# Differential attention: joining the two softmax halves one unit later, with scores one unit ahead

## The chip, the cores and the metric

The kernel runs on one core of a Trainium2 chip. The metric is the device time of one execution in microseconds (us). It is a whole two-layer network; the change lies in one phase of it, the attention of layer 0.

## The reference, cut to what matters

The network has two layers (layer 0 differential attention, layer 1 a state-space mixer), each followed by a dense MLP, over 1024 latent tokens and 256 context tokens. The attention has 8 heads; each head has two sets of queries and keys (c = 0, 1), two softmaxes, and one set of values:

```python
def attend(q, k, v):
    s = jnp.einsum('bqhcd,bkhcd->bhcqk', q, k).astype(jnp.float32)
    p = jax.nn.softmax(s, axis=-1)
    w = p[:, :, 0] - lam * p[:, :, 1]
    o = jnp.einsum('bhqk,bkhe->bqhe', w.astype(v.dtype), v)
    return rmsnorm(o, subln_g) * (1.0 - lambda_init)
```

Context queries see the 256 context keys, latent queries all 1280 keys. All is float32.

## The kernel before, in words

To keep float32 accuracy, products are done on TensorE (PE) with operands split into a high and a low part: `mm3` (lines 132 to 134) issues high x high, high x low and low x high. The split is a copy on ScalarE (ACT, L137) and a subtraction (L138) on VectorE (DVE) or GpSimd (POOL).

`phase_b` is the attention. A head is nine *units* of queries: u = 0 is the 256 context queries (two tiles of 128 with 256 keys each), u = 1 to 8 are 128 latent queries with 1280 keys each. Units pair up into five pairs of 256 queries: pair 0 is u = 0, pair 1 is u = 1 and 2, and so on to pair 4 (u = 7 and 8). The loop runs over n = 0 to 76: 72 units of eight heads, and five more to drain. In one turn of it several units are worked on:

- `scores` (L514, L520) of unit n: 12 matmuls (8 narrow ones for u = 0) into five banks of PSUM, half c = 0 in columns 0 to 1279, half c = 1 in 1280 to 2559.
- `maxima` (L529, L533) on DVE copies each half to SBUF (p0, p1) and takes its maximum; `exps` (L540, L543) on ACT does the exponentials in place, with their sums; `combine` (L551 to L554) on DVE joins the halves into p0. p0 has two buffers, p1 one.
- `w_part` transposes the joined weights of the unit before (`prev`) on PE (L566; L561 for u = 0) in three parts: four tiles into bank 5, two into the upper half of bank 6 (`pb`), four into bank 7, or bank 5 where a projection uses bank 7. `w_evac` brings them into wT: part 0 by ACT and DVE (L574, L575), parts 1 and 2 by a copy on ACT (L579) and a split on POOL (L580, L581).
- `values` of a pair: 30 matmuls (6 for pair 0) from wT and the values into the lower half of bank 6, once both units of the pair are in wT. The list `todo` sets when: two units after the pair's last unit. In these units (`late`) the evacuation is put behind the exponentials, since wT is still being read.
- `pair_out` (L662, L663) copies and squares the result; a unit later `pair_sums` (L669) sums the squares on PE into columns 256 and 257 of bank 6, which part 1 of the transposes also uses, and L670 copies them out.
- the projections of the next head's keys and queries, `proj_group`, in the units u = 0 (two), 2, 3, 5 and 7 (the table `AHEAD`): their 24 matmuls fill the gaps between the transposes (`fills`), in bank 7. Four are 512 columns wide, two 256. Afterwards come L466 on ACT and L467 on DVE (L461 and L462 for the narrow ones), a swap by DMA, POOL L472, DVE L475, and the split and store (L137, L138) some units later (`post`).
- norms of the head before the last (`norm_load`, `norm_calc`, `norm_rows`, `norm_pair` with L694), and for head 7 a part of the output product (`wo_group`) in ten units.

The order of PE, DVE, ACT and POOL within the phase is the order of the program text (`manual`). The DMAs are all issued on one queue (SP, line 80) whose order a scheduler chooses; a DMA there waits for its data, and those behind it wait with it. Keys have three buffers (`Kr`), queries two (`Qr`).

## Time and profile before

| what | us |
|---|---|
| three runs | 2940.19, 2940.97, 2946.08 |
| median | 2940.97 |
| profiled execution, first to last instruction (span) | 2929.2 |
| attention phase in the span (from the first scores of head 0) | 239.7 to about 907 |
| busy in the span: PE, DVE, ACT, POOL | 2739.6, 2021.3, 1367.5, 1062.1 |

The profile is of one execution; of that execution only the span is given. Matmuls are pipelined in the trace: a matmul's own time is longer than the distance to the next one's start, so durations on PE are read from starts. The profile's columns for a stretch of time are its length, the busy time of PE, the weight loads (PEld), DVE, ACT and POOL with the number of instructions, the clock granted to PE (1 is full), the share of DMA and its GB/s. In a timeline row stand start, duration, engine, line, operation, operands and count, and in brackets the idle time before it and who ended it.

### The profile page before, as it was taken

To read this page: it belongs to the slowest core of one execution; us is meant where nothing else is said; L and a number is where in the kernel's file an instruction comes from. 1 tells how busy PE (TensorE), PEld (TensorE's weight loads), DVE (VectorE), ACT (ScalarE), POOL (GpSimd) and SP (SyncE) were. 2 spreads that over 40 slices of the span, in tenths; PEclk is the share of its full clock that TensorE was granted. 3 is DMA by queue.
4 is the path that set the end of the run, shared out by engine and by line. 5 is a ranking of instruction groups with operands and counts; after the bars stand their busy time and mean duration, and the time that the engine had idled before them with its cause. 6 is when DMAs were issued, how large, how long until landed. Compare 5 with 4: busy or idle time off the path is not lost.

```text
span 2929.2 us, 43646 instructions
## 1 busy us (share of the span) xinstructions
PE 2739.6 (94%) x15200; PEld 2287.5 (78%) x15200; DVE 2021.3 (69%) x2956; ACT 1367.5 (47%) x2555; POOL 1062.1 (36%) x923
## 2 busy tenths in 40 slices
PE   5998999999988999999999999688899899999999
PEld 3687888788777887878877778588788678878887
DVE  5355777777764477676688768699743687758566
ACT  3424555555553663333444435377543643345443
POOL 2213666666553700000020004499410543326324
PEclk8999999999989999999999999899999999999999
DMA  9956455555744448886699988468834254467544
GB/s 250 292 181 205 139 164 169 162 149 162 220 145 152 140 152 303 303 291 243 228 299 293 274 241 258 153 200 264 282 124 136 72 175 159 148 213 256 159 139 141
DMA packets 454122, 588.44 MB, mean 201 GB/s; under 512 B 62742, under 2 KB 299532, under 8 KB 450700
## 3 DMA queue, kind: packets, MB, share of 16 engines
q1 hardware_dynamic: 453900, 585.63, 63.6%
q8 instruction: 120, 1.97, 0.3%
q14 instruction: 102, 0.84, 0.1%
HBM read 398.48 MB, written 182.82 MB: 198 GB/s over the span
## 4 chain that ended last, share of the span: by engine, by line
PE 66%; DMA 12%; DVE 10%; issue 4%; ACT 4%; SPq 2%; POOL 2%; DVEq 0%; ACTq 0%; POOLq 0%
PE PS L132 19%; PE PS L133 18%; PE PS L134 18%; SPq L80 2%; PE PS L520 2%; PE PS L1797 2%; ACT F L543 2%; PE PS L1832 1%; PE PS L566 1%; DVE F L533 1%; DVE R L138 1%; DVE H L138 1%; PE PS L202 1%; DMA U<-in_mlp_w 1%; DMA U<-Aa 1%
## 5 line engine op out<-in xcount | busy, mean ns | idle before, releaser
L132 PE MATMUL PS<-H 128*128 128x512 f32 x1048 | 412.0, 395 | 7.7 <-DVE FD L1604 5.0
L133 PE MATMUL PS<-H 128*128 128x512 f32 x1048 | 410.4, 392 | 0.0
L134 PE MATMUL PS<-H 128*128 128x512 f32 x1048 | 409.8, 392 | 0.0
L132 PE MATMUL PS<-H,R 128*128 128x512 f32 (+1 forms) x836 | 311.2, 378 | 18.5 <-ACT F L579 13.7
L133 PE MATMUL PS<-H,R 128*128 128x512 f32 (+1 forms) x836 | 303.8, 363 | 1.1 <-POOL H L138 1.1
L134 PE MATMUL PS<-H,R 128*128 128x512 f32 (+1 forms) x836 | 303.6, 364 | 0.0
L137 ACT ACTIVATE R<-W 128x512 fp32r<-128x512 f32 (+1 forms) x203 | 142.9, 711 | 208.7 <-PE PS L133 114.9
L132 PEld LDWEIGHTS PS<-H 128*128 128x128 f32 x1048 | 197.9, 189 | 52.4 <-DVE FD L1604 5.3
L134 PEld LDWEIGHTS PS<-H 128*128 128x128 f32 x1048 | 197.7, 189 | 42.5 <-issue 1.0
L133 PEld LDWEIGHTS PS<-H 128*128 128x128 f32 x1048 | 197.9, 189 | 41.2 <-issue 1.2
L132 PE MATMUL PS<-R,H 128*128 128x512 f32 x532 | 214.7, 407 | 7.4 <-ACT H L137 6.0
L543 ACT ACTIVATE F<-F,stat 128x1280 f32<-128x1280 f32 x128 | 174.3, 1362 | 83.8 <-DVE F L533 83.5
L133 PE MATMUL PS<-R,H 128*128 128x512 f32 x532 | 210.8, 397 | 0.0
L134 PE MATMUL PS<-R,H 128*128 128x512 f32 x532 | 208.3, 395 | 0.0
L137 ACT ACTIVATE H<-U 128x640 fp32r<-128x640 f32 x216 | 132.8, 677 | 144.2 <-PE PS L133 110.7
L132 PEld LDWEIGHTS PS<-H,R 128*128 128x128 f32 x836 | 160.7, 193 | 47.6 <-ACT F L579 15.1
L138 DVE TENSOR_TENSOR H<-W,H 128x512 fp32r<-128x512 f32 (+1 forms) x137 | 128.6, 949 | 93.6 <-ACT H L137 93.6
L138 DVE TENSOR_TENSOR R<-W,R 128x512 fp32r<-128x512 f32 (+1 forms) x166 | 150.8, 915 | 60.8 <-ACT R L137 53.5
L533 DVE TENSOR_SCALAR_CACHE_REDUCE F<-PS 128x1280 f32<-128x1280 f32 x128 | 185.1, 1482 | 9.1 <-PE PS L520 8.9
L138 DVE TENSOR_TENSOR H<-U,H 128x640 fp32r<-128x640 f32 x216 | 163.4, 793 | 39.5 <-ACT H L137 39.3
L580 POOL TENSOR_SCALAR R<-F 128x256 fp32r<-128x256 f32 (+1 forms) x128 | 122.8, 959 | 172.1 <-ACT F L579 149.1
L134 PEld LDWEIGHTS PS<-H,R 128*128 128x128 f32 x836 | 160.7, 192 | 25.9 <-issue 0.8
(477 smaller groups left out, 6818.0 us busy)
## 6 DMA issues: line engine op xcount, KB each, us to landing
W<-in_mlp_w SPq DMA_DIRECT2D x184, 256.0 KB, 3.1
U<-Aa SPq DMA_DIRECT2D x108, 320.0 KB, 5.0
Aa<-FU SPq DMA_DIRECT2D x91, 320.0 KB, 4.6
Ad<-F SPq DMA_DIRECT2D x112, 256.0 KB, 3.2
W<-Ad SPq DMA_DIRECT2D x112, 256.0 KB, 2.8
W<-in_ada_w SPq DMA_DIRECT2D x32, 512.0 KB, 6.9
FU<-in_mlp_w SPq DMA_DIRECT2D x32, 512.0 KB, 6.3
Ta<-FU SPq DMA_DIRECT2D x16, 1024.0 KB, 5.6
```

What stands on the lines that cost most here:

```text
L80: return self.nc.sync.dma_start(out=out, in_=in_)
L132: mm(out, ah, bh, start=first, stop=False, **kw)
L133: mm(out, ah, bl, start=False, stop=False, **kw)
L134: mm(out, al, bh, start=False, stop=last, **kw)
L137: self.nc.scalar.activation(hi, src, AF.Copy)
L138: (lo_eng or self.nc.vector).tensor_tensor(lo, src, hi.bitcast(F32), ALU.subtract)
L202: self.nc.tensor.matmul(acc[32 * j : 32 * j + 32, 0:256], self.scT[:, 2 * k : 2 * k + 32], w[:, 256 * j : 256 * j + 256], start=k == 0, st ...
L520: mm(self.PS[:, 1280 * c + k0 : 1280 * c + k1], Q[:, c, r, qs], K[c][:, k0:k1], start=r == 0, stop=r == 1)
L533: ts(p[c], self.PS[:, 1280 * c : 1280 * c + 1280], 1.0, None, ALU.mult, ALU.min, accum_out=sm[:, c : c + 1])
L543: nc.scalar.activation(p[c], p[c], AF.Exp, bias=sm[:, c : c + 1], scale=-1.0, accum_out=sn[:, 0:1] if c else s0[:, u + 1 : u + 2])
L580: nc.gpsimd.tensor_scalar(hi, t, 1.0, 0.0, ALU.mult, ALU.add)
L1797: mm(b[:, o : o + 160], X[:, d, i, 64 * j : 64 * j + 128], U[:, 4 * n + i, cols], start=True, stop=True)
```

## The change

- The joining of the halves (`combine`) of unit n moves to unit n + 1, ahead of that unit's maxima. The transposes move from one unit behind to two (`prevs`), the value products from n + 2 to n + 3, and the sums and norms with them by one unit; the loop has 78 turns in place of 77.
- `scores` of unit n + 1 stand at the end of turn n on PE, behind its transposes and fills, in place of those of unit n at its start.
- The evacuations stand in the same order in all units (`late` is gone).
- p0 has three buffers, keys have four, and the loads of keys and queries are put at other units to match. The two pools grow by 5 KB a partition each.

```diff
--- before.py
+++ after.py
@@ -616,13 +616,13 @@
 
     def phase_b(self):
         nc, mm = self.nc, self.nc.tensor.matmul
-        p0 = Ring([self.view(self.F1, 5 * i, (1280,)) for i in range(2)])
-        p1 = self.view(self.F1, 10, (1280,))
-        self.wraw = Ring([self.view(self.F1, 15 + 2 * i, (512,)) for i in range(3)])
+        p0 = Ring([self.view(self.F1, 5 * i, (1280,)) for i in range(3)])
+        p1 = self.view(self.F1, 15, (1280,))
+        self.wraw = Ring([self.view(self.F1, 20 + 2 * i, (512,)) for i in range(3)])
         o = self.fv(6, 256)
         sq = self.adat
         self.raw = Ring([self.wv(0, 1024)])
-        Kr = Ring([self.view(self.R1, 5 * i, (1280,)) for i in range(3)])
+        Kr = Ring([self.view(self.R1, x, (1280,)) for x in (0, 5, 10, 20)])
         Vr = Ring([self.rv(36 + 5 * i, 10, 128) for i in range(3)] + [self.view(self.R1, 15, (10, 128))])
         Qr = Ring([self.rv(51 + 4 * i, 2, 2, 256) for i in range(2)])
         self.wT = self.rv(16, 10, 256), self.rv(26, 10, 256)
@@ -630,7 +630,7 @@
         loaded = {}
 
         def load_k(h, c):
-            K = loaded[h, "k", c] = self.rv(0, 1280) if (h, c) == (7, 1) else Kr.next()
+            K = loaded[h, "k", c] = Kr.next()
             for k0, k1 in ((0, 256), (256, 1280)):
                 self.dma(K[:, k0:k1].bitcast(F32), self.Kd[h % 2, c, :, k0:k1])
 
@@ -753,8 +753,8 @@
             if u == 0:
                 self.oT = self.hgroups()
                 nc.vector.memset(ones, 1.0)
-            if u < 2:
-                wsplit6(u + 1)
+            if u in (0, 2):
+                wsplit6(u // 2 + 1)
             for g, k0, k1 in {0: ((2, 0, 6),), 1: ((0, 0, 3),), 2: ((0, 3, 6),), 3: ((1, 0, 3),), 4: ((1, 3, 6),)}.get(u, ()):
                 c0 = (256, 768, 0)[g]
                 for k in range(k0, k1):
@@ -786,7 +786,7 @@
         load_q(0, 1)
         load_v(0)
         units = [(h, u) for h in range(8) for u in range(9)]
-        prev, todo, sums, post, tail, run7 = None, [], [], [], [], []
+        prevs, joined, todo, sums, post, tail, run7 = [None, None], None, [], [], [], [], []
         split = self.proj_weights(1, 1)
         split(0)
         wts = {1: split(1)}
@@ -802,48 +802,54 @@
             while ready:
                 self.w_evac(*ready.pop(0))
 
+        def unit_args(h, u):
+            return u, loaded[h, (u + 1) // 2], (loaded[h, "k", 0], loaded[h, "k", 1])
+
         with self.manual():
-            for n in range(72 + 5):
+            self.scores(*unit_args(0, 0))
+            for n in range(72 + 6):
                 h, u = units[n] if n < 72 else (8, 9)
+                prev = prevs.pop(0)
                 front = n < 72
                 groups = []
                 pv = todo.pop(0)[1:] if todo and todo[0][0] == n else None
-                late = pv and pv[1]
                 parts = 3 if prev and prev[1] else 1 if prev else 0
-                if front and n - 6 >= 9 and (n - 6) % 9 < 5 and (n - 6) // 9 < 7:
-                    norm_load((n - 6) // 9 - 1, (n - 6) % 9)
+                if front and n - 7 >= 9 and (n - 7) % 9 < 5 and (n - 7) // 9 < 7:
+                    norm_load((n - 7) // 9 - 1, (n - 7) % 9)
                 if h == 7 and u > 5:
                     load6(u)
                 if front:
-                    K = loaded[h, 'k', 0], loaded[h, 'k', 1]
                     pair = (u + 1) // 2
-                    Q = loaded[h, pair]
                     s0 = hst[:, 0, h]
                     p, sn, sm = (p0.next(), p1), self.stat.next(), self.stat.next()
                     if u == 5 and h < 7:
                         load_v(h + 1)
                         load_k(h + 1, 0)
-                    if u % 2 == 0 and u < 8 and (h, pair + 1) not in loaded:
+                    if u == 6 and h < 7:
+                        load_k(h + 1, 1)
+                    if u in (1, 3, 5):
                         load_q(h, pair + 1)
+                    if u == 8 and h < 7:
+                        load_q(h + 1, 0)
+                        load_q(h + 1, 1)
                     if h < 7:
                         groups = [self.proj_group(h + 1, *a, wts[a[0]]) for a in self.AHEAD.get(u, ())]
                     if len(groups) == 2:
                         for f in groups[0][0] + groups[0][1]:
                             f()
-                    self.scores(u, Q, K)
-                    if u == 8 and h < 7:
-                        load_k(h + 1, 1)
-                        load_q(h + 1, 0)
-                        load_q(h + 1, 1)
+                if joined:
+                    self.combine(*joined)
+                    joined = None
+                if front:
                     self.maxima(u, p, sm)
-                if front:
+                    joined = u, p, s0, sn
                     if h < 7:
                         if u == 0:
                             qsplit = self.proj_weights(h + 1, 0)
                         if u == 5 and h < 6:
                             ksplit = self.proj_weights(h + 2, 1)
-                if 65 <= n < 75:
-                    groups = [wo_group(wo_order[n - 65])]
+                if 66 <= n < 76:
+                    groups = [wo_group(wo_order[n - 66])]
                 fills = [[], [], []]
                 if h >= 7 and groups:
                     fills = [groups[0][0][i : i + 2] for i in (0, 2, 4)]
@@ -856,27 +862,24 @@
                         tb = pb[:, 256:512] if part == 1 else self.bank(7 if part == 2 and not groups else 5)
                         t = self.w_part(prev[1], prev[2], part, tb)
                         ready.append((*t, part == 0))
-                    if not late or part == 2:
-                        evac()
+                    evac()
                     if part == 1:
                         next_post()
                     if front and part < 2:
                         self.exps(u, part, p, sm, s0, sn)
-                    if front and part == 1:
-                        self.combine(u, p, s0, sn)
-                    if late and part == 1:
-                        evac()
                     if part == 0:
                         todo7, run7 = run7, []
                         for f in todo7:
                             f.pop(0)()
                             if f:
                                 run7.append(f)
-                    if part == (2 if n < 73 else 0):
+                    if part == (2 if n < 74 else 0):
                         while sums and sums[0][0] <= n:
                             sums.pop(0)[1]()
                     for f in fills[part]:
                         f()
+                if n < 71:
+                    self.scores(*unit_args(*units[n + 1]))
                 if pv:
                     pair_out(*pv)
                     sums.append((n + 1, lambda a=pv: pair_sums(*a)))
@@ -894,17 +897,18 @@
                 if u == 8 and h < 6:
                     wts[1] = wk
                 if front and u % 2 == 0:
-                    todo.append((n + 2, h, pair))
-                prev = (h, u, p[0]) if front else None
+                    todo.append((n + 3, h, pair))
+                prevs.append((h, u, p[0]) if front else None)
                 if 0 < h < 8:
-                    if u == 3:
+                    step = u - 3 - (h < 7)
+                    if step == 0:
                         newton = norm_calc(h - 1)
-                    elif u == 4:
+                    elif step == 1:
                         newton()
-                    elif u == 5:
+                    elif step == 2:
                         norm_rows(h - 1)
-                if h < 8 and n - 6 >= 9 and (n - 6) % 9 < 5 and (n - 6) // 9 < 7:
-                    norm_pair((n - 6) // 9 - 1, (n - 6) % 9)
+                if h < 8 and n - 7 >= 9 and (n - 7) % 9 < 5 and (n - 7) // 9 < 7:
+                    norm_pair((n - 7) // 9 - 1, (n - 7) % 9)
                 if n == 72:
                     self.raw = Ring([self.wv(8, 1024), self.wv(12, 1024)])
                     self.wo_raws = [self.wo_load(3, 0), self.wo_load(0, 1)]
@@ -2227,7 +2231,7 @@
                     self.raw = Ring([self.wv(4 * i, 1024) for i in range(4)] + [self.f0(24.5 + 4 * i, 1024) for i in range(4)])
                     self.phase_v()
                 with pool("r1") as rp, pool("f1") as fp:
-                    self.R1, self.F1 = rp.tile([128, 20 * KB], F32R, name="R1"), fp.tile([128, 21 * KB], F32, name="F1")
+                    self.R1, self.F1 = rp.tile([128, 25 * KB], F32R, name="R1"), fp.tile([128, 26 * KB], F32, name="F1")
                     self.phase_b()
                 for g in range(3):
                     for j in range(2):
```

## The prediction

> **What bounds the kernel now.** I read the page's busy line first, then the busy time of each head of the attention phase, then the waits of TensorE (PE) in that phase, and last the timeline of two units, instruction by instruction. The diff touches only this phase; outside it the order on every engine of the built program is the same line for line.
>
> ```profile
> PE 2739.6 (94%) x15200; PEld 2287.5 (78%) x15200; DVE 2021.3 (69%) x2956; ACT 1367.5 (47%) x2555; POOL 1062.1 (36%) x923
> ```
>
> ```profile
> 239.66:312.75 73.09, 70.11 (x425) 61.20 (x425) 56.00 (x90) 42.72 (x82) 39.03 (x38) 0.98 0.49 152
> 312.75:392.23 79.48, 75.73 (x481) 67.62 (x480) 63.42 (x99) 46.42 (x92) 50.85 (x50) 0.98 0.50 148
> ...
> 724.61:803.88 79.27, 72.48 (x457) 63.39 (x455) 57.62 (x95) 41.27 (x86) 46.23 (x45) 1.00 0.72 220
> 803.88:907.00 103.12, 87.81 (x484) 74.46 (x485) 70.32 (x114) 55.43 (x108) 60.90 (x68) 0.92 0.40 125
> ```
>
> Each row runs from the first scores of one head to those of the next (columns: length, then PE, weight loads, DVE, ACT, POOL, clock). Head 0 takes 73.1 us, heads 1 to 6 together 803.88 - 312.75 = 491.1, so 81.9 each. PE is the bound and DVE the next: 63.4 of 79.5. With nine units in a head DVE needs about 7 us per unit, and that is what a unit costs when PE has little to do in it.
>
> ```profile
> PE PS L566 <- DVE R L575: 21.1, 14, 4.3
> PE PS L132 <- ACT F L579: 13.7, 6, 2.6
> PE PS L133 <- DVE R L575: 9.7, 6, 3.1
> PE PS L669 <- ACT F L579: 3.6, 1, 3.6
> ```
>
> These four waits, 48 us in 27 places, are nearly all that PE loses in the phase: transposes, projections and products that wait for a bank or for wT. They are also all that this change can win.
>
> ```profile
> 510.48 2.57 PE L520 MATMUL PS<-R,R 128*128 128x512 f32 x12
> 512.89 0.28 PE L132 MATMUL PS<-R 128*128 128x256 f32 x1
> ...
> 516.49 1.25 PE L566 MATMUL PS<-ident,F 128*128 128x128 f32 x10
> 517.50 2.57 PE L520 MATMUL PS<-R,R 128*128 128x512 f32 x12
> ...
> 521.26 0.66 PE L566 MATMUL PS<-ident,F 128*128 128x128 f32 x4 [1.19 <-DVE R L575]
> ...
> 526.59 0.50 PE L669 MATMUL PS<-lamc,adat 128*128 128x1 f32 x4
> 526.95 0.48 PE L132 MATMUL PS<-H,R 128*128 128x512 f32 x1
> ...
> 528.43 0.27 PE L684 MATMUL PS<-ident,FC 128*10 128x128 f32 x1
> ...
> 554.63 0.39 PE L132 MATMUL PS<-H,R 128*128 128x256 f32 x1 [2.50 <-ACT F L579]
> ...
> 557.60 1.12 PE L514 MATMUL PS<-R,R 128*128 128x256 f32 x8
> ```
>
> Starts give the prices on PE: scores of a unit 2.41 us (510.48 to 512.89), the 30 value products of a pair 3.60, ten transposes 1.01, sums 0.36 (526.59 to 526.95). From 521.26 to 528.43 one unit with a wide projection passes: 7.17, of which transposes 1.01 and sums 0.36, so 5.8 for the projection; a 256-column projection takes 2.97 (554.63 to 557.60). A head's sum: scores 8 x 2.41 + 1.0, values 4 x 3.60 + 0.7 for the short pair, transposes 8.5, wide projections 4 x 5.8, narrow 2 x 2.97, sums 1.8, together 74.8 us. The other 7 us of the 81.9 are the waits.
>
> **The change, part by part.** *Where the work lies.* Before, a pair's value products run two units after its last unit, in u = 2, 4, 6, 8 and 1; the projections lie in u = 0, 2, 3, 5, 7. So a unit has one or the other, and PE's load is even. The change moves the products one unit on (n + 3): u = 3, 5, 7, 0, 2. Now every unit with products also has a projection, and u = 1, 4, 6, 8 have neither: PE has 2.41 + 1.01 + 0.36 = 3.8 us in them. Scores a unit ahead could bridge this only if DVE and ACT could also finish such a unit in 3.8 us. They can't:
>
> ```profile
> 521.12 1.10 DVE L138 TENSOR_TENSOR R<-FC,R 128x512 fp32r<-128x512 f32 x1
> ...
> 523.67 1.37 ACT L543 ACTIVATE F<-F,stat 128x1280 f32<-128x1280 f32 x1 [1.11 <-DVE F L533]
> 525.03 0.36 ACT L579 ACTIVATE F<-PS 128x256 f32<-128x256 f32 x1
> ...
> 528.63 0.60 ACT L466 ACTIVATE FC<-PS 128x512 f32<-128x512 f32 x1 [1.13 <-PE PS L134]
> 529.26 0.69 DVE L467 SCALAR_TENSOR_TENSOR FC<-PS,W 128x512 f32<-128x512 f32 x1
> 530.14 1.49 DVE L533 TENSOR_SCALAR_CACHE_REDUCE F<-PS 128x1280 f32<-128x1280 f32 x1 [0.19 <-PE PS L520]
> 531.56 1.49 DVE L533 TENSOR_SCALAR_CACHE_REDUCE F<-PS 128x1280 f32<-128x1280 f32 x1
> 531.68 1.37 ACT L543 ACTIVATE F<-F,stat 128x1280 f32<-128x1280 f32 x1 [2.31 <-DVE F L533]
> 534.58 0.16 DVE L551 RECIPROCAL stat<-stat 128x1 f32<-128x1 f32 x1 [1.52 <-ACT F L543]
> 536.50 0.68 DVE L575 TENSOR_TENSOR R<-PS,R 128x512 fp32r<-128x512 f32 x1
> 537.40 0.55 DVE L694 SCALAR_TENSOR_TENSOR W<-W,lamc 128x256 f32<-128x256 f32 x1 [0.22 <-DMA W<-rsd]
> ```
>
> *The new wait.* Let S be the start of the light unit's scores on PE, which is the end of the projection before it. Then in order: ACT L466, and 0.63 us later DVE L467 (528.63 to 529.26), 0.69 long. Behind it on DVE, by the new order, stands `combine` of the unit before (534.58 to 536.50: 1.9; I take 2.0), then the maxima. The exponential can start 1.54 after the first maximum starts (530.14 to 531.68); behind it on ACT the copy of the second transposes starts 1.36 later (523.67 to 525.03) and takes 0.36. That copy frees the half bank into which `pair_sums` writes, the sums now lie in the light units (products a unit before), and on PE they stand ahead of the next unit's scores. Sums 0.36. Together 0.63 + 0.69 + 2.0 + 1.54 + 1.36 + 0.36 + 0.36 = 6.94, with the release 7.0. So u = 6 and u = 4 (there L462 and a late exponential stand in for L467) take 7.0 in place of 3.8. In u = 1 and u = 8 the unit before also leaves L138 (1.10) and L694 (0.55) to DVE; L138 fills the wait for L466, the rest is late by 1.2: 8.2.
>
> That this wait is real is seen once in the trace, in the one unit (head 7, u = 0) that already has neither products nor a projection:
>
> ```profile
> 803.88 0.51 PE L514 MATMUL PS<-R,R 128*128 128x256 f32 x2 [0.56 <-DMA H<-on]
> ...
> 815.39 0.98 PE L669 MATMUL PS<-lamc,adat 128*128 128x1 f32 x4 [3.57 <-ACT F L579]
> 816.23 2.48 PE L520 MATMUL PS<-R,R 128*128 128x512 f32 x6
> ```
>
> It lasts 12.35 us, with 3.57 of waiting for that very copy: the upper bound of a light unit. The lower bound, if the sums did not wait and only the second maximum held the scores back, is 0.63 + 0.69 + 2.0 + 2 x 1.42 (530.14 to 531.56) = 6.2, less the first four score products, say 5.3.
>
> *Scores a unit ahead, join later, third p0 buffer.* These take the join off the way to the transposes and the scores off the way to the maxima. They remove the waits above (the 14 waits of L566 and the 6 of L133 have a whole unit's slack now), and the sum below books all units with a projection at PE's own time: a full gain. What is late next there: in u = 3 the third transposes wait for L575, which stands behind the maxima: S + 1.35 + 1.2 + 2.0 + 2.96 + 0.68 = 8.2, then 0.7 for transposes and sums: 8.9 in place of 7.45. POOL's last split of wT ends some 1 to 2 us before the products need it, so it costs nothing; uncovered it would cost 1 us a pair.
>
> *Keys in four slots, queries.* Keys are loaded in u = 5 and 6, hidden under two units. The next head's first queries are not: their scores now come at the end of u = 8, while the load stands in the same place of SP's queue, behind projection swaps, stores and norm loads.
>
> ```profile
> 544.97 2.47 PE L520 MATMUL PS<-R,R 128*128 128x512 f32 x12
> ...
> 553.73 1.79 SPq L80 DMA_DIRECT2D R<-Qd  x3
> ```
>
> It was issued 8.8 us after the scores of u = 8 and used 3.9 later (557.60), 12.6 in all. DVE's part comes about 2 us earlier now, so I take 10.2 for u = 8, that is 2.0 more than its chain; the bounds are 0 and 4.4.
>
> *Clock.*
>
> ```profile
> 468.30:471.70 3.40, 0.90 (x7) 0.79 (x7) 1.98 (x4) 2.83 (x6) 1.24 (x1) 0.97 0.50 150
> 471.70:475.10 3.40, 3.40 (x18) 3.40 (x18) 0.92 (x2) 0.00 (x0) 3.23 (x5) 0.52 0.70 246
> ```
>
> After a stretch of 3.4 us in which PE worked 0.9, the clock stands at half for the next 3.4 us. The light units make four such gaps (3.2 to 6.4 us) in each head. Half clock costs between 0 (it falls into the gap) and 3.4 / 2 = 1.7; I take 0.85 each. The wait of 2.5 before 554.63 brought no such drop, the one above did.
>
> The Trainium skill, "TensorE: Matmul & The Clock Gate", Part 1, has the clock go to half after at least one idle window of about 3.4 us. The trace disagrees in part: the window above was not wholly idle, and it dropped. By the skill's rule only u = 1 and u = 8 could drop, and the sum would be 12 us lower.
>
> *The sum*, u = 0 to 8: 1.0 + 2.97 + 3.60 + 1.01 + 5.8 = 14.4; 8.2; 12.2; 8.9; 7.0; 12.8; 7.0; 12.8; 10.2. Together 93.5, with clock 96.9, which is 15.0 over 81.9. Six heads: +90. Head 0 has no products in u = 0 and 2 (7.2 less), no L694 (1.4 less) and less ahead of the queries (1.5 less): 86.8 against 73.1; its first units have no light predecessor, so I take +11. Head 7 keeps its output products in each unit but gets one more unit without them, and the phase one unit more: 0 to +10, I take +4. In all +105 us on the profiled span of 2929.2. The runs' median, 2940.97, lies 11.8 above that span; I carry this over: **3046 us**.
>
> **Rivals.** (1) *The waits go and nothing comes in their place.* PE's 48 us of waits vanish, perhaps a few more: 2941 - 55 = 2886. For it speaks that all four waits are for things the change gives a unit more time; against it, the light units. It wins if DVE's and ACT's chain after a projection takes under 3.8 us; the rows say 7. (2) *Smaller loss*: the clock holds (24 less) and light units come near the lower bound (1.7 less, four times seven: 48): 3046 - 72 = 2974. The Trainium skill's rule on idle windows (same section) would be half of the clock part. (3) *Larger loss*: light units behave as the unit at 803.88. Then 4 x (12.35 - 3.8) = 34 on 74.8, +27 a head, 3046 + 7 x 12 = 3130. For it: that is a measured light unit; against it: DMA for head 7 ran beside it, and 4.3 us of it was a wait for a bank that the new order removes. That the change doesn't do what it says can be left out: the order of these four engines is written by hand.
>
> **Chances.** Forecast (2985 to 3085): 0.74. Larger: 0.10. Smaller but still slower: 0.09. Faster: 0.05, same: 0.02. The range takes chain 1 us off per light unit (28), clock 0 (24), query wait 0 (14), partly together: 61 down; up, clock 1.7 (24), `combine` beside POOL 0.4 longer (11): 39. The bound for "same" is 0.2%, about 6 us, twice what the runs of before differ in the middle.
>
> **What would show it.** In the profile after: PE idle before L669 (the sums), released by ACT L579 (the copy), in some 28 places of 2 to 4 us; little left of L566 waiting for L575; heads of 93 to 100 us; light units of 7 to 8 us between score starts against 12 to 15 in the others; first scores of a head (L514) waiting for the query load; half-clock windows by the dozen. It would be wrong if light units take under 5 us, or if the heads stay at or under 82.

## The result, and the profile after

The changed kernel takes 3096.43 us (median of four runs, 3095.49 to 3101.0), the kernel before 2940.58 beside it: ratio 1.0538, 95% interval 1.0517 to 1.0558. It is slower, as forecast, but by 156 us and not 105; the time lies 11 us above the range.

From the page of the profile after: the first line, the busy line, and TensorE's granted clock in the 40 slices.

```profile
span 3094.9 us, 43675 instructions
...
PE 2799.7 (90%) x15200; PEld 2339.2 (76%) x15200; DVE 2028.7 (66%) x2956; ACT 1366.5 (44%) x2555; POOL 1050.5 (34%) x923
...
PEclk8998888888888999999999999989999999999999
```

The same row of the kernel before:

```profile
PEclk8999999999989999999999999899999999999999
```

The work is the same; PE's share fell from 94% to 90%, and the clock is lower in nine slices of the attention (behind it, one low slice lies one place further on). The waits of PE in that phase (microseconds in all, places, longest):

```profile
PE PS L669 <- ACT F L579: 137.8, 28, 11.1
PE PS L566 <- DVE R L575: 12.3, 9, 1.7
PE PS L514 <- DMA R<-Qd: 9.7, 1, 9.7
PE PS L520 <- DVE F L533: 3.1, 1, 3.1
```

The sums wait for the copy of the second transposes in 28 places, the number foretold. That the number fits exactly is partly luck: 27 of them lie in the light units of heads 0 to 6 and last 4.7 us each, where 2 to 4 were foretold. These units are 28, but the first has no sums yet; the 28th wait, of 11.1 us, lies in head 7 (at 989.37). The old waits of the projections and the products are gone; that of L566 for L575 fell from 21.1 us to 12.3. The only wait for the queries of a head is at the start of the phase. By stage (head 0; heads 1 to 6; then one head from u = 0 to u = 8, each row from the start of the unit's scores to that of the next; columns as before):

```profile
241.06:334.86 93.80, 75.27 (x391) 64.92 (x391) 56.39 (x86) 40.44 (x75) 30.29 (x32) 0.86 0.40 126
334.86:966.52 631.66, 506.59 (x2875) 445.32 (x2876) 395.34 (x602) 279.31 (x565) 298.10 (x301) 0.89 0.45 133
```

```profile
649.90:665.70 15.80, 15.80 (x98) 14.67 (x99) 5.71 (x15) 5.79 (x19) 5.80 (x8) 0.88 0.64 166
665.70:675.89 10.19, 4.44 (x27) 3.80 (x26) 8.93 (x14) 4.93 (x9) 5.38 (x7) 0.91 0.51 142
675.89:690.09 14.20, 14.20 (x71) 12.47 (x72) 8.50 (x11) 5.39 (x12) 6.01 (x6) 0.82 0.54 172
690.09:699.31 9.22, 7.55 (x58) 7.02 (x56) 7.40 (x10) 5.03 (x9) 4.22 (x4) 1.00 0.64 184
699.31:707.72 8.41, 4.10 (x29) 3.49 (x28) 7.04 (x10) 4.17 (x11) 5.50 (x7) 1.00 0.43 119
707.72:721.90 14.18, 14.18 (x78) 12.39 (x78) 7.95 (x13) 6.36 (x13) 4.91 (x6) 0.88 0.36 112
721.90:729.78 7.88, 4.43 (x28) 3.83 (x26) 6.24 (x9) 3.91 (x6) 4.77 (x6) 0.93 0.41 116
729.78:745.50 15.72, 15.36 (x78) 12.89 (x79) 6.23 (x9) 6.44 (x15) 7.56 (x8) 0.82 0.07 10
745.50:755.70 10.20, 4.50 (x28) 3.82 (x27) 8.95 (x11) 4.99 (x9) 6.56 (x7) 0.85 0.51 146
```

Heads 1 to 6 take 631.66 / 6 = 105.3 each, against 81.9. Read the second row of the unit table: PE is busy 4.4 of 10.2 us while DVE is busy 8.9; in the long units it is the reverse. The clock column shows the second loss: the long units, where PE hardly waits, run at 0.82 to 0.88. One light unit (u = 8) in the timeline:

```profile
639.76 2.49 PE L520 MATMUL PS<-R,R 128*128 128x512 f32 x12
...
640.04 1.81 DVE L138 TENSOR_TENSOR R<-FC,R 128x512 fp32r<-128x512 f32 x1 [4.37 <-ACT R L137]
...
641.96 0.69 DVE L467 SCALAR_TENSOR_TENSOR FC<-PS,W 128x512 f32<-128x512 f32 x1
...
642.57 1.26 DVE L694 SCALAR_TENSOR_TENSOR W<-W,lamc 128x256 f32<-128x256 f32 x1
...
643.75 0.15 DVE L551 RECIPROCAL stat<-stat 128x1 f32<-128x1 f32 x1
...
644.19 1.55 DVE L554 SCALAR_TENSOR_TENSOR F<-F,stat 128x1280 f32<-128x1280 f32 x1
...
645.66 1.48 DVE L533 TENSOR_SCALAR_CACHE_REDUCE F<-PS 128x1280 f32<-128x1280 f32 x1
...
647.19 1.36 ACT L543 ACTIVATE F<-F,stat 128x1280 f32<-128x1280 f32 x1 [2.42 <-DVE F L533]
...
648.55 0.36 ACT L579 ACTIVATE F<-PS 128x256 f32<-128x256 f32 x1
...
649.06 0.99 PE L669 MATMUL PS<-lamc,adat 128*128 128x1 f32 x4 [5.70 <-ACT F L579]
```

This is the chain of the prediction: DVE has no gap from 640.04 to the end of the maxima, the joining (643.75 to 645.66) stands between the projection's leftovers and the maximum, and PE stands 5.70 us for a 0.36 us copy.

### The profile page after: what moved, and what is told of

Read it like the earlier page. It is cut to its first block, busy times and chain, and to the rows that moved or that the text cites. A ratio compares the mean times of both kernels' runs of the same rounds, so it can differ in the third digit from the quotient of the medians.

```text
span 3094.9 us, 43675 instructions
## 1 busy us (share of the span) xinstructions
PE 2799.7 (90%) x15200; PEld 2339.2 (76%) x15200; DVE 2028.7 (66%) x2956; ACT 1366.5 (44%) x2555; POOL 1050.5 (34%) x923
## 3 DMA queue, kind: packets, MB, share of 16 engines
q8 instruction: 120, 1.97, 0.3%
## 4 chain that ended last, share of the span: by engine, by line
PE 66%; DMA 12%; DVE 9%; issue 5%; ACT 3%; POOL 2%; SPq 2%; DVEq 0%; ACTq 0%; POOLq 0%
PE PS L132 18%; PE PS L133 18%; PE PS L134 18%; PE PS L520 3%; DMA FU<-in_mlp_w 2%; SPq L80 2%; PE PS L1801 2%; PE PS L1836 1%; DVE F L554 1%; DMA Ta<-FU 1%; DMA W<-in_ada_w 1%; DVE R L138 1%; PE PS L566 1%; PE PS L669 1%; ACT F L543 1%
## 5 line engine op out<-in xcount | busy, mean ns | idle before, releaser
L132 PE MATMUL PS<-H 128*128 128x512 f32 x1048 | 412.4, 395 | 2.7 <-ACT H L137 2.7
L132 PE MATMUL PS<-H,R 128*128 128x512 f32 (+1 forms) x836 | 309.1, 375 | 1.7 <-DVE R L462 0.9
L132 PEld LDWEIGHTS PS<-H 128*128 128x128 f32 x1048 | 198.1, 189 | 47.7 <-issue 3.8
L132 PE MATMUL PS<-R,H 128*128 128x512 f32 x532 | 213.4, 404 | 4.5 <-ACT H L137 2.5
L520 PE MATMUL PS<-R,R 128*128 128x512 f32 (+1 forms) x768 | 202.5, 424 | 3.1 <-DVE F L533 3.1
L138 DVE TENSOR_TENSOR H<-U,H 128x640 fp32r<-128x640 f32 x216 | 163.4, 793 | 48.2 <-ACT H L137 47.2
L138 DVE TENSOR_TENSOR R<-W,R 128x512 fp32r<-128x512 f32 (+1 forms) x166 | 150.3, 913 | 66.7 <-ACT R L137 58.6
L138 DVE TENSOR_TENSOR H<-W,H 128x512 fp32r<-128x512 f32 (+1 forms) x137 | 127.5, 942 | 97.8 <-ACT H L137 96.7
L580 POOL TENSOR_SCALAR R<-F 128x256 fp32r<-128x256 f32 (+1 forms) x128 | 81.6, 637 | 317.1 <-ACT F L579 295.9
L133 PEld LDWEIGHTS PS<-H,R 128*128 128x128 f32 x836 | 162.6, 195 | 27.9 <-POOL H L138 6.8
```

What stands on the lines that cost most here:

```text
L132: mm(out, ah, bh, start=first, stop=False, **kw)
L133: mm(out, ah, bl, start=False, stop=False, **kw)
L138: (lo_eng or self.nc.vector).tensor_tensor(lo, src, hi.bitcast(F32), ALU.subtract)
L520: mm(self.PS[:, 1280 * c + k0 : 1280 * c + k1], Q[:, c, r, qs], K[c][:, k0:k1], start=r == 0, stop=r == 1)
L580: nc.gpsimd.tensor_scalar(hi, t, 1.0, 0.0, ALU.mult, ALU.add)
```

## The experiments

Theory A: the light units' chain on DVE and ACT sets their time, link by link, with the joining the largest; half clock in the next unit comes with the gaps. Rival B: products and projections that meet in the same units cost this whatever the chain. Rival C: half clock is the main loss. In the recorded expectations the letters mean something else: there theory A is the meeting of products and projections, with the light units that it leaves, and theory B is the chain over the joining, wherever the products and projections lie.

Each group of runs had the kernel before beside it, with medians from 2930 to 2943 us, so times from different groups are best compared by their ratios.

| kernel | us | ratio to the kernel before, interval |
|---|---|---|
| before_proj_later | 3003.90 | 1.0223, 1.0207 to 1.0239 |
| after_proj_later | 3059.28 | 1.0423, 1.0402 to 1.0444 |
| after_proj_earlier | 3048.18 | 1.0351, 1.0334 to 1.0368 |
| after_gap_filled | 3049.38 | 1.0377, 1.0346 to 1.0407 |
| after_own_join | 2991.46 | 1.0188, 1.0170 to 1.0205 |
| after_prod_back | 3123.44 | 1.0628, 1.0593 to 1.0663 |
| after_sums_last | 3092.94 | 1.0529, 1.0487 to 1.0572 |
| own_join_sums_last | 2981.98 | 1.0151, 1.0118 to 1.0184 |
| own_join_proj_later | 3013.47 | 1.0258, 1.0226 to 1.0290 |
| own_join_proj_earlier | 3013.59 | 1.0243, 1.0226 to 1.0260 |
| own_sums_proj_earlier | 3043.83 | 1.0346, 1.0330 to 1.0361 |
| own_join_gap_filled | 2973.35 | 1.0121, 1.0096 to 1.0147 |
| join_in_long | 3000.91 | 1.0218, 1.0192 to 1.0243 |
| join_in_long_copy_first | 2971.03 | 1.0118, 1.0097 to 1.0140 |
| light_copies_first | 2985.41 | 1.0186, 1.0167 to 1.0204 |
| light_copies_norm_later | 2961.61 | 1.0111, 1.0094 to 1.0129 |
| chain_shortest | 2937.98 | 0.9997, 0.9980 to 1.0013 |
| squares_earlier | 2932.04 | 0.9992, 0.9977 to 1.0007 |

**Moving the projections.** The kernel before with its projections one unit later, so that it too has them with the products; and the changed kernel with them one later, so that they meet no longer. The loads of keys and queries and the splits of weights move with them. In both, weights of the output product for two heads are loaded over a rotation table that the last projection still reads; own_join_proj_later below loads them a unit later, and why it too computes other values was not traced. The instruction counts are the same.

```diff
-    AHEAD = {0: ((1, 2), (1, 0)), 2: ((1, 1),), 3: ((0, 2),), 5: ((0, 0),), 7: ((0, 1),)}
+    AHEAD = {1: ((1, 2), (1, 0)), 3: ((1, 1),), 4: ((0, 2),), 6: ((0, 0),), 8: ((0, 1),)}
...
```

> The mirror: the kernel before, with only the projections one unit later, so that here they meet the products (u = 1, 4, 6, 8), while join, scores and transposes stay as they were. Theory A: light units in u = 0, 2, 5, 7, half-clock stretches, heads of 90 to 100 us, 2990 to 3080 us. Theory B: no change beyond 10 us from 2941.

> The changed kernel with the projections of the next head one unit later (u = 1, 3, 4, 6, 8), so that they lie in the units without products. Theory A (units with products and projections at once leave four light units, in which the chain DVE, ACT, copy, sums sets the pace): the light units go, heads come to 75 to 80 us, the time to 2880 to 2930 us. Theory B (the join ahead of the next maxima and the longer way itself cost, wherever the projections lie): 3040 us or more.

The mirror costs 66 us (the kernel before beside it took 2937.86), and its largest wait of PE is the same one, in 27 places, in a kernel that has none of the diff:

```profile
PE PS L669 <- ACT F L579: 54.6, 27, 3.0
```

So the meeting is enough to make the wait, at 2.0 a place; in the diff's order it is 4.7. But parting them in the changed kernel won only 37 us, far from the 2880 to 2930 us that the meeting alone would give. New waits came: L566 for L575 53.9 us in 34 places, and the scores for late queries (22.7) and for L694 (21.6). The other direction, one unit earlier, also in two kernels that join in the own unit (the projected keys and queries of some heads are then not the reference's, why was not traced; the instruction counts are the same):

```diff
-    AHEAD = {0: ((1, 2), (1, 0)), 2: ((1, 1),), 3: ((0, 2),), 5: ((0, 0),), 7: ((0, 1),)}
+    AHEAD = {1: ((1, 1),), 2: ((0, 2),), 4: ((0, 0),), 6: ((0, 1),)}
...
+                        if n == 0 or u == 8 and h < 6:
+                            groups = [self.proj_group(h + 2 - (n == 0), 1, g, wts[1]) for g in (2, 0)]
...
```

> The changed kernel with the projections one unit earlier (u = 8 of the head before, 1, 2, 4, 6), again out of the units with products, but with queries and keys stored earlier than before, so that no load is late. Theory A (meeting of products and projections alone): 2890 to 2940 us. Theory B (the chain over the join ahead of the maxima is the larger part): 3000 to 3040 us, with PE waiting in the third transposes for DVE's subtraction.

> Join in its own unit and projections one unit later, all else as changed. Theory A alone: no light unit is left and the join is off the chain, 2870 to 2930 us. If the other waits seen with later projections (the third transposes for DVE's subtraction, 54 us, and the queries, 23 us) stay although the join no longer stands ahead of them: 2960 to 3030 us.

> Both undone: join in its own unit, projections one unit earlier; scores ahead, transposes two units on, products three units on stay. If join and placement together make the loss: PE has 74.8 us of work a head and few waits, heads of 77 to 81 us, 2890 to 2935 us, no slower than the kernel before. If something else of the change (longer way, the order with products first) costs: 2960 or more.

> The same with the sums behind the scores. With no light units the sums should have little to wait for: within 10 us of the run with both undone.

after_proj_earlier lies above both of its ranges. With the joining in the own unit both directions are about 20 us slower than without moving anything, and the last, with the sums moved too, slower still by 30 where 10 at most was expected; this was not explained. In the earlier kernels the first products of u = 8's projections wait for weights that POOL has not split yet, here in own_join_proj_earlier:

```profile
PE PS L134 <- POOL R L138: 27.0, 6, 4.5
```

A moved projection brings its weights, its evacuation and its stores with it, so these runs could not settle B: each trades one wait for another.

**The clock.** The third transposes are repeated in the light units, so that PE's gaps are filled with work that changes nothing.

```diff
+                        if part == 2 and h < 7 and u in (1, 4, 6, 8):
+                            for _ in range(9 if u in (4, 6) else 14):
+                                self.w_part(prev[1], prev[2], part, tb)
```

> The changed kernel with the third transposes of the light units repeated (9 times in u = 4 and 6, 14 times in u = 1 and 8), so that PE works through most of its wait; the chain and the results are the same. If the half clock after the gaps costs what the long units show (14.2 + 15.8 + 14.2 + 15.8 against 52.3 us by starts at full clock, so 7.7 us a head): 3035 to 3055 us, with hardly a half-clock stretch. If the longer units have another cause: 3096, or more by what the repeats cost.

It wins 47 us with more work. The light units u = 6, 8 and 1 nearly keep their length (7.7, 9.9 and 9.9 us), and u = 4 takes 8.4 in two of five heads and 9.3 in the others; the long units u = 5, 7, 0 and 2 are back at full clock:

```profile
577.45:590.11 12.66, 12.66 (x79) 11.17 (x79) 7.48 (x12) 5.63 (x11) 3.97 (x6) 1.00 0.39 126
597.82:611.21 13.39, 13.03 (x80) 11.19 (x80) 6.04 (x9) 6.67 (x15) 7.83 (x8) 1.00 0.04 11
621.12:635.45 14.33, 14.33 (x98) 13.07 (x98) 5.41 (x15) 6.01 (x19) 6.23 (x8) 1.00 0.59 185
645.37:657.29 11.92, 11.92 (x72) 10.61 (x72) 8.88 (x11) 5.86 (x12) 6.62 (x6) 1.00 0.56 182
```

Together 52.3, in place of 15.80 + 14.20 + 14.18 + 15.72 = 59.9. The clock is a third of the loss, not its main part: C falls.

**The links.** First the joining alone, back in its own unit behind the second exponential; all else of the change stays.

```diff
-                if joined:
-                    self.combine(*joined)
-                    joined = None
...
                         self.exps(u, part, p, sm, s0, sn)
+                    if front and part == 1:
+                        self.combine(u, p, s0, sn)
```

> The changed kernel with one part undone: the halves are joined in their own unit, behind the second exponential, as before; scores ahead, transposes two units on and products where the change has them. If the join ahead of the maxima is a link of the light units' chain (1.9 us each): light units of 6 to 8.3 us and 3096 less 4 x 1.9 x 8 = 61, 3020 to 3050 us. If the chain does not run over it: within 10 us of 3096.

105 us back, two thirds of the loss, from one position in DVE's queue; light units of 5.8 to 7.8 us. That is more than the 61 expected, since less is lost to the clock too: with the gaps filled in both (after_gap_filled and, below, own_join_gap_filled) the joining makes 76 us (3049.38 and 2973.35). Then the sums, moved on PE behind the next unit's scores (with the joining where the change put it, and in the own unit), and the transposes and products a unit back with the late joining kept:

```diff
-                    if part == (2 if n < 74 else 0):
+                    if part == 0 and n >= 74:
...
                     self.scores(*unit_args(*units[n + 1]))
+                if n < 74:
+                    while sums and sums[0][0] <= n:
+                        sums.pop(0)[1]()
```

```diff
-        prevs, joined, todo, sums, post, tail, run7 = [None, None], None, [], [], [], [], []
+        prevs, joined, todo, sums, post, tail, run7 = [None], None, [], [], [], [], []
...
-                    todo.append((n + 3, h, pair))
+                    todo.append((n + 2, h, pair))
```

> The changed kernel with the sums of squares behind the next unit's scores on PE, not ahead of them. If the sums' wait for the copy is what holds PE in the light units: scores start some 2 us earlier there, 4 x 2 x 8 = 64 us less and fewer half-clock stretches, 3000 to 3040 us. If scores would wait for the second maximum as long: within 20 us of 3096.

> Join in its own unit and sums behind the scores, all else as changed. The join alone gave 2991 us, with 58 us of PE's waits at the sums left, 13 more of them laid to POOL. If these go: 2905 to 2945 us, about the kernel before or better. If another wait takes their place: 2970 to 2991.

> The changed kernel with another part undone: transposes one unit on and products two units on, as before, so that products and projections lie in different units again; the join stays in the next unit ahead of its maxima, scores stay ahead. Theory A (the meeting of products and projections makes the loss): 2900 to 2970 us. Theory B (the chain over the join sets the pace wherever products lie; the transposes now wait for it too): over 3020 us. Both at work: between.

Taking the sums out of the way wins 4 us, which is within the intervals: the scores behind them then wait for the maxima, the link before the copy in the same chain.

```profile
PE PS L520 <- DVE F L533: 68.2, 29, 5.7
PE PS L514 <- DVE F L533: 25.6, 7, 3.8
```

With the joining gone from the chain the same edit wins 9, and there too the intervals overlap. And a late joining with early transposes makes PE wait for the joining itself, 119.9 us in 37 places: the joining and the transposes had to move together.

What was left, some 50 us over the kernel before, could still be chain or clock. Three kernels: the gaps of after_own_join filled (4 and 6 repeats); the joining deferred only from light units into the long ones; and, with that, the second copy ahead of the exponentials in light units.

```diff
                         self.exps(u, part, p, sm, s0, sn)
+                    if joined and part == 1 and u not in (1, 4, 6, 8):
+                        self.combine(*joined)
+                        joined = None
```

```diff
-                        self.exps(u, part, p, sm, s0, sn)
+                        light = h < 7 and parts == 3 and u in (1, 4, 6, 8)
+                        for c in ((), (0, 1))[part] if light else (part,):
+                            self.exps(u, c, p, sm, s0, sn)
...
```

> Joining in the own unit everywhere (2991), and in the light units the third transposes are repeated 4 times (u = 4, 6) or 6 times (u = 1, 8) to fill PE's gaps with work that changes nothing. If half clock still takes its share there (15 to 25 us at the rate that filling the changed kernel's gaps gave), 2973 (2966 to 2980). If what is left over the kernel before is all the waiting itself, 2991 within 6.

> The joining stays ahead of the maxima for the light units u = 1, 4, 6 and 8 (it then runs in the following, long unit), and is done in its own unit behind the second exponential in all others, so that no light unit has a joining ahead of its maxima and none has one of its own. If the length of DVE's and ACT's chain in the light units sets the time, and DVE has room in the long units: at least what joining in the own unit everywhere gave (2991), about 2978 (2965 to 2993), with light units of 5 to 6.5 us. If a joining ahead of the maxima costs in long units too, it comes out over 3000.

> As the one before, and in the light units ACT's copy of the second part of the transposes (L579) stands ahead of the first exponential, so that the sums no longer wait for the exponential. The light unit's chain is then L466 0.6, L467 0.7, two maxima 3.0, about 4.5 to 5 us beside 3.8 of PE work. If the chain theory holds: waits of L669 for L579 under 15 us, light units of 4.5 to 6 us, time 2950 (2930 to 2970), near the kernel before or under it. If the wait merely goes to the maxima, as when the sums were put behind the scores: 2975 or more, with L520 waiting for L533.

The clock's share was 18 us, as worked out. join_in_long missed (3001, not 2978): no light unit has a joining any more, but the copy still stands behind the exponential, and the wait did not move (58.9 us in 22 places; after_own_join 58.3 in 22). One ACT position earlier for the copy, and it is a fifth of that; the time, 2971.03, lies 1 us above its range, and the sums now wait for POOL, 17.3 us in 13 places:

```profile
PE PS L132 <- ACT FC L670: 13.6, 10, 1.9
PE PS L669 <- ACT F L579: 11.4, 15, 5.8
```

The first line is what came next: u = 0's first projection uses the bank of the third copy, which now stands behind both exponentials (the wait is put down to L670, the next on ACT behind that copy). The following kernels take such links in turn: light_copies_first puts the third copy ahead too, and the exponentials and the joining of u = 2, 5, 7 directly behind the maxima; light_copies_norm_later also moves the scaling L694 from the end of a turn to behind its exponentials; chain_shortest takes u = 5 and 7 back and puts L694 ahead of the joining; squares_earlier puts u = 3's sums and squares forward.

```diff
+                    if early and part == 0:
+                        self.exps(u, 0, p, sm, s0, sn)
+                        self.exps(u, 1, p, sm, s0, sn)
                     evac()
...
+                    if front and not early:
+                        for c in ((), (), (0, 1))[part] if light else (part,) if part < 2 else ():
+                            self.exps(u, c, p, sm, s0, sn)
...
+                if pend:
+                    norm_pair(*pend)
+                    pend = None
...
```

> As join_in_long_copy_first (2971; a head of 85.4 us from 571.29 to 656.66, of which u = 0 lost 1.8 to the first projection waiting for ACT behind the exponentials, and u = 3 1.4 to the joining of u = 2 at the end of its unit). Here the third copy too stands ahead of the exponentials in the light units, and in u = 2, 5 and 7 both exponentials and the joining follow the maxima at once. If these two waits go: 3 us a head less, 2950 (2940 to 2960). If the chain merely turns to another link: 2965 or more.

> As light_copies_first, and the scaling of the head before (norm_load and norm_pair, L694) is moved from the end of a turn to behind its exponentials, so that it is no longer ahead of the maxima of u = 1 and u = 3. Worth 1.3 in u = 1 (5.9 beside 4.4 in u = 6 and 8) and 0.5 in u = 3: 10 to 12 us less than light_copies_first, about 2938 (2925 to 2952). That is at the kernel before; under 2930 it would be faster. If POOL's work, not L694, holds u = 1: the same as light_copies_first.

> From light_copies_norm_later (2962; a head of 84.2 us) two links are put back or forward that its trace names: u = 5 and u = 7 do their exponentials and joining where join_in_long_copy_first had them (there u = 5 took 12.8 in place of 14.5, and u = 8 4.4 in place of 5.4, since the projection's addition L475 no longer stands behind the joining), and the scaling L694 stands ahead of the joining in u = 3, so that u = 4 loses 0.8. By the rows of the two runs a head takes 14.2 + 4.5 + 12.6 + 8.9 + 5.1 + 12.8 + 4.4 + 14.0 + 4.5 = 81.0, as against 81.9 in the kernel before: 2939 (2928 to 2952), no longer to be told from the kernel before. If the meeting of products and projections costs by itself, the light units may be short and the time still stays over 2952.

> From chain_shortest (2938, level with the kernel before): in u = 3 the sums stand behind the first transposes and the copy and squares of the pair's output (L662, L663) ahead of the third copy, so that in u = 4 the sums no longer wait for the squares (8.0 us in 6 places, 1.4 the longest) and POOL has them done a unit earlier. If that wait goes and nothing takes its place: 5 to 8 us less, 2931 (2924 to 2938), a ratio of 0.997 to the kernel before. If another link of u = 4 (the copy of the second transposes) is as late: the same as chain_shortest.

The first missed: u = 5 grew from 12.8 to 14.3 and u = 8 from 4.4 to 7.1. In u = 7 the projection's addition L475 now stood behind the joining, so that its split came late into u = 8; chain_shortest, which takes this back and puts L694 ahead of the joining, has u = 8 short again and u = 5 too in most heads. The second won 24 us where 10 to 12 were expected: u = 1 fell from 5.9 to 4.5, but u = 8 too, from 7.1 to 5.4, and u = 0 from 15.6 to 14.2. It is still above its range, since its base was. chain_shortest came out as expected, level with the kernel before; of its units, u = 1, then 4 to 8 and 0:

```profile
571.00:575.42 4.42, 4.02 (x28) 3.41 (x26) 4.08 (x5) 2.77 (x7) 4.20 (x6) 1.00 0.80 232
...
596.53:602.10 5.57, 4.16 (x29) 3.49 (x28) 5.30 (x7) 4.08 (x11) 5.11 (x6) 1.00 0.84 255
602.10:614.73 12.63, 12.63 (x78) 11.15 (x78) 10.55 (x19) 6.89 (x14) 5.94 (x8) 1.00 0.54 160
614.73:619.15 4.42, 4.02 (x27) 3.41 (x26) 4.28 (x5) 2.06 (x5) 4.34 (x4) 1.00 0.32 89
619.15:632.90 13.75, 13.17 (x79) 11.17 (x79) 10.25 (x15) 8.17 (x16) 9.00 (x10) 1.00 0.19 49
632.90:637.32 4.42, 4.02 (x27) 3.41 (x26) 4.16 (x6) 2.77 (x7) 4.34 (x5) 1.00 0.50 124
637.32:651.48 14.16, 14.16 (x99) 13.04 (x98) 9.31 (x25) 7.89 (x21) 7.35 (x10) 1.00 0.71 216
```

Light units of 4.42 us, and 5.57 for u = 4, against 7.9 to 10.2, the clock at 1.00, with products and projections still in the same units. B falls as a cost of its own: what the meeting does, it does through the chain. Heads 1 to 6 of this kernel, then of the kernel before:

```profile
314.81:798.12 483.31, 460.89 (x2877) 400.86 (x2876) 382.99 (x602) 278.67 (x564) 289.05 (x301) 1.00 0.58 173
```

```profile
312.75:803.88 491.13, 454.81 (x2852) 401.49 (x2850) 380.14 (x598) 277.43 (x558) 311.83 (x298) 0.99 0.57 168
```

They are 7.8 us shorter than before, in one execution each. Head 7 starts 5.8 earlier (798.12), and the first product of the phase behind the attention (L132 on RT) 1.4 earlier (925.45 against 926.80): head 7 and the drain with the extra unit, to which most of these edits do not apply, cost 4.4 more. The span ends 4.4 later all the same; those 5.8 us arise behind the attention, where nothing was changed, and are less than the spread between executions of one kernel (2929.69 to 2950.82 for the kernel before beside it).

The time of squares_earlier, 6 us under chain_shortest, looks like the gain that was expected, but it is mostly the group's: the kernel before beside them took 2940.47 and 2936.04, and by the ratios 1.5 us are left, well inside both intervals. Its trace shows why. In u = 4 the wait for the squares is gone, and the unit fell from 5.57 to 4.49 us, but u = 3 grew from 8.3 to 9.1 and u = 5 from 12.6 to 13.7; a new wait of 7.5 us in 6 places stands before L566. No version was measurably faster than the kernel before.

## Why the prediction was right or wrong

The mechanism was right: the light units, the wait of L669 for L579, and the joining as the link that makes it long. The gain that the change was good for, PE's old waits, came in the main, and was as small as said: of 48 us, 12 stayed (L566, in u = 3 above all, where the prediction had it). Of the working, two terms in each head were mis-sized, and one was too small in head 0. By spans: 165.7 us were lost, 105 predicted.

- **The clock term failed in size.** 3.4 us a head was predicted, 0.85 for each gap; the four long units lost 59.9 - 52.3 = 7.6. The bound given, 1.7 each, is 6.8, and was passed too. It counts one stretch of 3.4 us at half clock behind each gap. In the trace half clock begins inside the gap in u = 8 and u = 1, so that a part of it is free, as the prediction allowed; but behind three of the four gaps (u = 8, 1 and 6) it lasts two such stretches, here in u = 8, whose sums start at 649.06, and the unit behind it:

```profile
643.40:646.80 3.40, 0.00 (x0) 0.00 (x0) 3.33 (x5) 0.90 (x2) 2.12 (x2) 1.00 0.80 221
646.80:650.20 3.40, 1.14 (x5) 1.18 (x6) 2.37 (x5) 3.01 (x6) 1.12 (x2) 0.50 0.53 152
650.20:653.60 3.40, 3.40 (x17) 3.40 (x17) 0.78 (x1) 1.02 (x4) 2.71 (x4) 0.50 0.60 146
```

The four pure lengths, 14.4, 12.2, 12.8 and 12.8, were right in sum, 52.2; measured are 14.3, 11.9, 12.7 and 13.4, so the errors, 0.6 at most in u = 7, cancel by luck.
- **The Trainium skill's rule**, in "TensorE: Matmul & The Clock Gate", Part 1, asks for a whole idle window of about 3.4 us. The first row above fits it: PE does nothing in it, and the clock drops. By it only u = 1 and u = 8 could drop the clock with the predicted gaps, and the runs speak against that. In u = 4 PE works 0.97 us in the 3.41 before the drop (704.84 to 708.25). In after_own_join the unit below, u = 4, has PE idle for 6.27 - 4.10 = 2.2 us, and the one behind it runs at 0.88:

```profile
631.64:637.91 6.27, 4.10 (x28) 3.49 (x28) 6.02 (x10) 4.15 (x11) 5.50 (x6) 1.00 0.74 229
637.91:652.09 14.18, 14.18 (x78) 12.39 (x78) 10.25 (x16) 6.37 (x13) 6.19 (x6) 0.88 0.40 122
```

- **The light units were put 4.6 us a head too short, and their chain 6.6.** u = 1, 3, 4, 6 and 8 were put at 8.2, 8.9, 7.0, 7.0 and 10.2, and took 10.2, 9.2, 8.4, 7.9 and 10.2; the 10.2 put for u = 8 held 2.0 for a wait that never came. The failed step is to take each duration from one row of the old unit: L138 was 1.10 and L694 0.55 there, and in u = 8 here, beside POOL's splits, 1.81 and 1.26; and L138 does not fill the wait for L466, it holds L467 back. The trace of the kernel before could have warned: over its attention L138 on this shape takes from 0.68 to 1.74, and L694 from 0.47 to 1.42. The range allowed only `combine` 0.4 longer for work beside POOL; put at 2.0, it takes 1.9 in u = 8, 2.2 in u = 6 and 2.9 in u = 4. The sums at half clock took 0.84 (649.06 to 649.90), not 0.36.
- **The query load did not cost 2.0 in u = 8.** That wait appears nowhere but at the start. u = 8 came to 10.2 because of L138 and L694, as u = 1 did: right for the wrong reason.
- **Head 0** lost 93.8 - 73.1 = 20.7, not 11. Of that, 2.1 are a matter of the boundary: the old row starts at 239.66, inside the first scores, which begin at 237.55. Another 4.9 are the first narrow projection. It ran ahead of the first scores, while the queries were being loaded (227.50 to 230.5), and now stands behind them, at half clock after that wait (243.27 to 248.1); the prediction left this move out. Its first units have no light predecessor, but the clock of the whole head fell to 0.86 all the same. Head 7 and the rest lost 4.5 where 4 was taken.
- **From span to median** 11.8 us were carried over from the kernel before. Here the median lies 1.5 above the span.

These close the account. Clock and light units, 4.2 and 4.6, are 8.8 in the head shown, which with 105.8 us is 0.5 longer than the mean. By the mean, 8.4 more in each of six heads, 9.7 in head 0 and 0.5 in head 7 are 60.6, less 10.3 for the carry, and 3046 + 50.3 = 3096.3. The range's upper side held the clock's bound in full (24 us) but only 11 for a longer chain, where 4.6 in six heads make 28, and nothing for head 0.

Of the rivals, the larger loss (3130) came nearer than the smaller, and nearer than the forecast itself, but not by its reason: its light unit of 12.35 us did not come in heads 1 to 6. Only head 7 has one like it, u = 1 with neither projection nor output product, and that took 16.1 us (974.16 to 990.22), 11.1 of them the wait for the copy. The faster rival's condition, a chain under 3.8 us, was never met; at 4.4 us, in chain_shortest, the change is level.

## What to carry to other kernels

Where each engine works through its program in order, as here, an operation that nobody waits for yet still delays all that stands behind it: before moving one "out of the way", list what it is put ahead of, and ask for each of those who is waiting. When work is regrouped so that one engine has full and nearly empty units, time the other engines' chain in the empty ones, with the spread of durations that the old trace shows beside different neighbours, not one row of each. A chain is mended link by link, in the order the trace names them, and each mend is judged by what becomes late next.

## What the runs showed of the hardware

The same DVE subtraction of 128x512 (L138, R from FC and R) took from 0.68 to 1.74 us within the attention of the kernel before, and from 0.69 to 1.81 in the kernel after and in chain_shortest. In the five places of these three traces where no POOL instruction ran beside it, it took 0.68 or 0.69. POOL's 128x256 subtraction (L138, W) took from 0.73 to 1.97 within the kernel after. The first two rows are of chain_shortest, the others of the kernel after; the 1.81 of DVE shown above (640.04) lay beside a POOL subtraction of 1.30 that began at 640.01:

```profile
571.23 0.69 DVE L138 TENSOR_TENSOR R<-FC,R 128x512 fp32r<-128x512 f32 x1 [0.54 <-ACT R L137]
571.25 1.81 POOL L581 TENSOR_TENSOR R<-F,R 128x512 fp32r<-128x512 f32 x1
...
644.19 1.55 DVE L554 SCALAR_TENSOR_TENSOR F<-F,stat 128x1280 f32<-128x1280 f32 x1
644.36 1.97 POOL L138 TENSOR_TENSOR W<-W 128x256 fp32r<-128x256 f32 x1 [0.81 <-ACT W L137]
```

The Trainium skill, "SBUF — State Buffer", in its part on the two separate sides, says that DVE and GpSimd share a port pair which one of them holds for a whole instruction. The rows fit this in direction: one of the two keeps its length, and the other ends later by about its own. POOL ends 0.6 after DVE in the last two rows, near its own 0.74, and 1.1 after it in the first two, near 1.30. No run here took the neighbour away alone, so it is read from rows and not shown.

Filling gaps with useless transposes made two kernels faster, by 47 and by 18 us. In own_join_gap_filled the light units kept their lengths (5.8 to 7.8 us) and it is the long ones behind them that became shorter, u = 2 from 13.5 to 12.0 and u = 5 from 14.2 to 13.1, at a clock of 1.00: the gain is the clock's.
